# A decoder step on one core: the convolution's state transposed in by 4 blocks of 88 rows and out by 5, in place of 22 and 22

## The chip, the core and the metric

The kernel runs on 1 core of one Trainium2 chip. The core has a matrix engine (TensorE, PE in the rows; PEld is its weight load), three engines for elementwise work (VectorE is DVE, ScalarE is ACT, GpSimd is POOL) and a queue engine that issues transfers (SyncE, SP). Matrix products land in PSUM, everything else lies in SBUF. The metric is the time of one execution on the device in microseconds.

## What is computed

One inference step of a single decoder layer for a prompt of 512 tokens and 8 sampled sequences of 8 tokens (576 tokens together): RMSNorm, one input projection that feeds retention heads and dilated attention heads, an output projection with residual, RMSNorm, a gated feed-forward with a causal depthwise convolution of width 3, and a last RMSNorm. The part that the change touches is the feed-forward with its convolution state:

```python
    h = _rmsnorm(x, norm2_w)
    ua, ub = jnp.split(h @ w_up, [D_FF], axis=-1)
    buf = jnp.concatenate([conv_s0.astype(ua.dtype), ua], axis=1)
    conv = conv_b
    for j in range(CONV_W):
        conv = conv + buf[:, j:j + T] * conv_w[j]
    x = x + (jax.nn.silu(conv) * ub) @ w_down
    return (x, ret_s.astype(ret_s0.dtype), k_all[:, -keep:], v_all[:, -keep:], buf[:, -(CONV_W - 1):])
```

`conv_s0` is `state_conv`, 8 sequences of 2 rows of 2816 features (zero for the prompt). The last two rows of `buf` are an output: 2 rows for the prompt, 16 for the samples.

## The kernel before, in words

Activations are kept with features on the 128 partitions and the 576 tokens along the free side. So 2816 features are 22 tiles (`NF`), numbered f. Every large product goes through `dense` (line 245): for each k tile of the contraction it issues six matmuls (line 254), three passes (high part by high part, high by low, low by high) over two halves of 288 tokens. Weights come 128 columns at a time into `wraw` (three buffers, loaded by SP, line 211), ScalarE makes the high part `whi` (line 219) and VectorE the low part `wlo` (line 229), two buffers each; VectorE's subtraction is what frees a `wraw` buffer for the next load.

The order of work on TensorE is written by `Merge` (line 96) at build time. Each piece of work is a generator that yields an estimated cost and a latency; a stream comes up again once the planner's clock has passed its latency. One k step of `dense` counts 738 ns on that clock. So a stream that yields a latency of 7600 is continued after 11 k steps, one that yields 25000 after 34. Once built, the order is fixed: an engine waits at an instruction whose input is late, and all that is queued behind it on that engine waits too.

When attention and retention are done, the tiles of the last phase are allocated (lines 1018 to 1027) and two streams begin: `conv_state_in` and `rest`, which is `out_proj` (8 tiles of columns, m = 0 to 7, 8 k steps each, with `out_post` behind each) and then `feed_forward` (up f = 0 to 10, down 0 to 7, up f = 11 to 21, down 0 to 7). The first of the new tiles to be filled are `nfw` (line 1285, a 512 KB load) and `csn` (line 1051, the state), both issued by SP ahead of the weights of out tiles m = 3 to 7.

`conv_state_in` loads the state as 16 rows of 2816 floats. 22 transposes of 16 x 128 (line 1055) put it into one PSUM tile, and one VectorE copy (line 1056) brings it to `csT`, [128 features, f, 16]. `up_post` (line 1116) copies a slice of `csT` into the work buffer `ue` on POOL (line 1121), and copies the last two columns of each sequence into `cout` on POOL (lines 1127 and 1128). In the same POOL queue stands the product of gate and convolution (line 1141), which waits for VectorE (line 1138). `conv_state_out` starts in the second run of down products: 22 transposes of `cout[:, f]`, 128 x 18 (line 1160), in groups of four, a VectorE copy behind each group (line 1161), and two stores by SP (lines 1163 and 1164). In `down_post`, `rows_out` transposes the final rows, five transposes for each tile of columns (line 1170).

Of the kernel before, what the change touches and what calls it, by code (L numbers as in the profile page):

```python
# [10 lines left out]
F32 = mybir.dt.float32  # L11
# [7 lines left out]
P = 128  # L19
# [76 lines left out]
class Merge:  # L96
    """Interleaves streams of tensor-engine work.

    A stream is a generator; it yields (cost, latency): what its last burst holds the tensor engine for,
    and how long the other engines then take before its next burst can start.  A third number, if given,  # L100
    takes the place of the cost in the pace.  None: it waits for another stream.  Streams with work
    left advance in proportion to it; a stream without goes first as soon as it is ready."""

# [43 lines left out]
def decoder_step(ctx, tc, a):  # L147
# [14 lines left out]
    def room(n):  # L162
        """n of the small tiles of PSUM are free from here on; give() returns them when their readers are issued"""
        while held[0] + n > 4:
            yield None
        held[0] += n

    def give(n):
        held[0] -= n
# [6 lines left out]

    # ---- weights, streamed in order of use
    def wsrc(w, m, k0, k1):
# [66 lines left out]
    def dense(ps, key, xhi, xlo, k0, k1, first, last, rows=None, made=None):  # L245
        """ps[:, C0 + n] (+)= sum over k of w[k, cols]^T x[k, n], in three exact-split passes."""
        i, (hi, lo) = w_next(key)
        w_split_hi(i + 1)
        for k in range(k0, k1):
            while made is not None and k not in made:  # L250
                yield None
            for wt, x in ((hi, xhi), (hi, xlo), (lo, xhi)):
                for s in range(2):
                    pe.matmul(ps[:, C0 + s * H2:C0 + (s + 1) * H2], wt[:, rows[k] if rows else k - k0], x[k][:, s * H2:(s + 1) * H2],  # L254
                              start=first and k == k0 and wt is hi and x is xhi,
                              stop=last and k == k1 - 1 and wt is lo)
            if k == k0 + 1:
                w_split_lo(i + 1)
            if k == k0 + 3:
                w_load(i + 4)  # L260
            yield 738.0, 0.0
# [3 lines left out]

    # ---- constants
    ident = cst.tile([P, P], F32, name="ident")
# [30 lines left out]
    def rsqrt_steps(dst, v, t):  # L298
        """dst = v ** -0.5 for positive v: a seed from the exponent, then Newton's steps; t: scratch."""
        dve.tensor_scalar(dst.bitcast(I32), v.bitcast(I32), -0.5, 1597463007.0, op0=OP.mult, op1=OP.add)  # L300
        for _ in range(3):
            yield 0.0, 700.0
            dve.tensor_mul(t, dst, dst)
            dve.scalar_tensor_tensor(t, t, -0.5, v, op0=OP.mult, op1=OP.mult)
            dve.scalar_tensor_tensor(dst, t, 1.5, dst, op0=OP.add, op1=OP.mult)
# [17 lines left out]

    # ================= first norm
    def halves():
# [113 lines left out]
    def in_first():  # L439
        """the first two tiles of columns advance together as x arrives"""  # L440
        ps = [dtile() for _ in range(2)]
# [32 lines left out]

    # ================= input projection, retention and dilated attention, by pairs of heads
    mid = ctx.enter_context(ExitStack())
# [12 lines left out]
    def natural(src, dst):  # L489
        """dst [token, tile, 128] = the transpose of src [128 features, T]"""  # L490
        yield from room(2)
        p1, p2 = mtile(), mtile()
        for j in range(5):
            r, s = rows_of(j)
            pe.transpose((p1[:, s] if j < 4 else p2[:NS, :P]), src[:, s], ident)  # L495
        yield 550.0, 300.0
        act.copy(dst[:, 0:4], p1.rearrange("p (j c) -> p j c", j=4))
        dve.tensor_copy(dst[:NS, 4], p2[:NS, :P])
        give(2)
# [91 lines left out]

    # ---- retention
    sbds, s0s, qms = [], [], []
# [11 lines left out]
    def retention():  # L605
        for hp in range(4):
# [5 lines left out]
            for h2, q in halves():  # L612
# [6 lines left out]
                               onehot[:NS, None, :, None].to_broadcast([NS, 2, B, DH]), op=OP.mult)  # L619
            # scores, transposed: [key, query]  # L620
            at = rp.tile([P, 2, 4, P], F32, name="at", tag="at", bufs=1)
# [17 lines left out]
            yield 2 * 216.0, 0.0  # L639
            # states after each chunk  # L640
            yield from room(1)
# [10 lines left out]
            for h2, q in halves():  # L652
                act.activation(st[q], pS[q, q], AF.Copy, scale=fin[q, 0, hp:hp + 1])
            # outputs
            give(1)
# [19 lines left out]
            yield 6 * 216.0, 0.0  # L675
            # group norm; the decay of a row only scales its statistics
            g = gst[hp % 2]
# [25 lines left out]
            for r_, n0, n1_, ps in parts:  # L703
                dve.tensor_mul(cen[:r_, n0:n1_], cen[:r_, n0:n1_],
                               g2[:r_, n0:n1_].unsqueeze(2).to_broadcast([r_, n1_ - n0, DH]))
            # states of the sample group
            yield from room(1)
# [9 lines left out]
            act.activation(sn, sn, AF.Copy, scale=fin[:, 1, hp:hp + 1])  # L717
            # gate
            yield from room(2)
# [11 lines left out]

    # ---- dilated attention, prompt
    half, used = {}, {}
# [7 lines left out]
    def attn_unit(hp, i):  # L741
        """128 queries of two heads, from their scores in PSUM on"""
        n = (i + 1) * P
        S, PT = [], []
        if i:
            # the scores in two passes: [q hi; q hi] with [k hi; k lo], then q lo with k hi
            q_ = A[hp][4][:, i * P:(i + 1) * P]
# [70 lines left out]
    def k_split(hp):  # L818
        """[k hi; k lo] of each head"""
        k_ = A[hp][5]  # L820
# [24 lines left out]

    # ---- dilated attention, sample: four sequences at a time, each in 32 columns of the tensor engine
    kvb = []
    SW = SK + NS

    def attn_sample():  # L850
# [3 lines left out]
        def load(u, x, which):  # L854
            """the 768 rows of a cache that some query of the window reads, for a pair of heads"""
            hp, g = units[u]
# [25 lines left out]
        def unit(u):  # L882
# [19 lines left out]
            dve.tensor_scalar(s[:, :SK], s[:, :SK], c[:, 2:3], None, op0=OP.mult)  # L902
            # the weights of the new tokens, each sequence's in its own 8 of the 64 columns
            dve.tensor_tensor(s[:, SK:].rearrange("p (b t) -> p b t", b=B),
# [95 lines left out]
    kvb.append(kvx.enter_context(tc.tile_pool(name="kv", bufs=2, reuse_waits="tile")))  # L1000
    # the mixed heads take the place of x, in the order in which the output projection takes them
    MIX = [4, 5, 6, 7, 0, 1, 2, 3]
# [13 lines left out]

    # ================= output projection, second norm
    fp = ctx.enter_context(tc.tile_pool(name="ffn", bufs=1, reuse_waits="tile"))
# [4 lines left out]
    csT = fp.tile([P, NF, 16], F32, name="csT")  # L1023
    cout = fp.tile([P, NF, 18], F32, name="cout")
    nfw = fp.tile([P, D], F32, name="nfw")
# [23 lines left out]
    def conv_state_in():  # L1049
        csn = fp.tile([18, DFF], F32, name="csn", tag="co", bufs=1)  # L1050
        sp.dma_start(csn[:16], a["state_conv"].rearrange("b j f -> (b j) f"))
        yield 0.0, 7600.0
        ps = mtile()
        for f in range(NF):
            pe.transpose(ps[:, f * 16:(f + 1) * 16], csn[:16, f * P:(f + 1) * P], ident[:16, :16])
        dve.tensor_copy(csT.rearrange("p f j -> p (f j)"), ps[:, :NF * 16])
        cs_made.append(1)
        yield 1400.0, 4300.0

# [33 lines left out]

    # ================= feed-forward
    ues = []
# [20 lines left out]
    def up_post(f, pa, pb, done, ghi, glo, made):  # L1116
# [9 lines left out]
        act.activation(c[:, :L], u[:, 0:L], AF.Identity, scale=convw[:, 0, f:f + 1], bias=convb[:, f:f + 1])  # L1126
        pool.tensor_copy(cout[:, f, 0:2], u[:, NP:NP + 2])  # L1127
        pool.tensor_copy(by_seq(cout[:, f, 2:]), seqs(u, TS, 2))
        yield 0.0, 1800.0
# [22 lines left out]
    def conv_state_out():  # L1152
        co = fp.tile([18, DFF], F32, name="co", tag="co", bufs=1)
        while len(up_made) < NF:
            yield None
        for f0 in range(0, NF, 4):
            ps = mtile()
            n = min(4, NF - f0)
            for f in range(f0, f0 + n):
                pe.transpose(ps[:18, (f - f0) * P:(f - f0 + 1) * P], cout[:, f], ident)  # L1160
            dve.tensor_copy(co[:, f0 * P:(f0 + n) * P], ps[:18, :n * P])
            yield n * 110.0, 300.0
        sp.dma_start(a["o_conv_p"][0], co[0:2])
        sp.dma_start(a["o_conv_s"].rearrange("b j f -> (b j) f"), co[2:18])

# [30 lines left out]
    def last_down(ghi, glo, yn):  # L1196
        """the last tile of columns, one group of tokens after the other, so that the first one's norm runs beside the second"""
        m, k0 = KD - 1, NFH
# [124 lines left out]
```

## Time and profile before

| what | value |
|---|---|
| runs shown | 839.37 us median of 3 (834.9 to 840.41) |
| profiled execution, first to last instruction | 838.0 us |
| PE busy | 817.6 us (98%) |
| PEld busy | 775.0 us (92%) |
| DVE busy | 414.1 us (49%) |
| ACT busy | 295.2 us (35%) |
| POOL busy | 148.4 us (18%) |
| PE's share of the chain that ended last | 92% (72% is line 254) |

The median stands 1.37 us over the profiled span; launch and end, which lie around the span, are in it. The rows shown further down come from the same execution. A row of the timeline or of the chain gives the start in us, the length in us, the engine, the line, the operation with out<-in, and how many instructions are merged; an idle time ahead of it stands in brackets with what ended it. Ends of matmuls are modelled, so distances from start to start are the safer measure on PE.

### The profile page before, as it was taken

The page shows a single profiled execution, that of the slowest core. Times are in us where ns is not written, and L with a number is a line of the kernel's source. Part 1 is how long each engine was busy: PE and PEld are TensorE (multiplying, and loading weights), DVE is VectorE, ACT ScalarE, POOL GpSimd, SP SyncE. Part 2 cuts the span into 40 slices and gives each one's busy share as a digit, 9 for nine tenths or more (in the row PEclk, how much of TensorE's full clock was granted, in tenths as well). Part 3 has the DMA queues.
Part 4 walks back from the last instruction along what each step waited for, and adds up shares of the span by engine and source line. Part 5 has one row for each costly group of instructions (what it writes and reads, how often), then busy time and mean ns, then how long its engine had stood idle before and what let it go on. Part 6 is the DMA issues. An engine that isn't in the chain of part 4 may idle for free.

```text
span 838.0 us, 16048 instructions
## 1 busy us (share of the span) xinstructions
PE 817.6 (98%) x6594; PEld 775.0 (92%) x6594; DVE 414.1 (49%) x796; ACT 295.2 (35%) x511; POOL 148.4 (18%) x234
## 2 busy tenths in 40 slices
PE   7999999998999999999999999999999999999995
PEld 6999999886887888999999999999999999999995
DVE  5664655655556456544555455432235545545333
ACT  5322321544536367234223333311223323332222
POOL 1312111020111113022212222100012222210111
PEclk9999999999999999899999999999999999999999
DMA  9355562667796873555256544453334445553213
GB/s 268 104 167 163 162 201 70 184 187 217 201 251 184 237 201 85 109 176 169 84 179 198 176 158 138 135 170 87 94 101 156 146 152 176 170 169 81 70 51 114
DMA packets 179534, 128.68 MB, mean 154 GB/s; under 512 B 15425, under 2 KB 176101, under 8 KB 178914
## 3 DMA queue, kind: packets, MB, share of 16 engines
q1 hardware_dynamic: 178308, 93.75, 40.1%
q10 hardware_dynamic: 928, 33.63, 11.0%
q8 instruction: 52, 0.85, 0.4%
q0 software_dynamic: 224, 0.28, 0.1%
q14 instruction: 22, 0.18, 0.1%
HBM read 121.52 MB, written 39.66 MB: 192 GB/s over the span
## 4 chain that ended last, share of the span: by engine, by line
PE 92%; DMA 3%; DVE 1%; ACT 1%; SPq 1%; issue 1%; POOL 0%; ACTq 0%; DVEq 0%; POOLq 0%
PE d L254 72%; PE m L877 2%; PE d L451 2%; PE m L923 2%; DMA kc<-in_cache_win_k_dram 1%; PE m L791 1%; PE d L887 1%; PE m L495 1%; PE m L804 1%; PE px L410 1%; PE m L1213 1%; PE px L254 1%; DMA csn<-in_state_conv_dram 1%; PE m L663 1%; PE m L764 1%
## 5 line engine op out<-in xcount | busy, mean ns | idle before, releaser
L219 ACT ACTIVATE whi<-wraw 128x1024 fp32r<-128x1024 f32 (+2 forms) x114 | 110.8, 972 | 372.2 <-issue 182.1
L229 DVE TENSOR_TENSOR wlo<-wraw,whi 128x1024 fp32r<-128x1024 f32 (+2 forms) x114 | 126.8, 1112 | 119.8 <-ACT whi L219 116.8
L254 PE MATMUL d<-bhi,whi 128*128 128x288 f32 x768 | 174.6, 309 | 0.0
L254 PE MATMUL d<-bhi,wlo 128*128 128x288 f32 x768 | 165.0, 297 | 0.0
L254 PE MATMUL d<-blo,whi 128*128 128x288 f32 x768 | 164.8, 296 | 0.0
L254 PE MATMUL d<-hhi,whi 128*128 128x288 f32 x704 | 150.9, 296 | 0.0
L254 PE MATMUL d<-hlo,whi 128*128 128x288 f32 x704 | 150.8, 296 | 0.0
L254 PE MATMUL d<-hhi,wlo 128*128 128x288 f32 x704 | 150.7, 296 | 0.0
L254 PEld LDWEIGHTS d<-bhi,whi 128*128 128x128 f32 x768 | 122.4, 191 | 5.3 <-issue 3.6
L254 PEld LDWEIGHTS d<-bhi,wlo 128*128 128x128 f32 x768 | 124.1, 189 | 0.0
L254 PEld LDWEIGHTS d<-blo,whi 128*128 128x128 f32 x768 | 124.1, 190 | 0.0
L254 PEld LDWEIGHTS d<-hhi,whi 128*128 128x128 f32 x704 | 113.4, 189 | 0.1
L254 PEld LDWEIGHTS d<-hhi,wlo 128*128 128x128 f32 x704 | 113.4, 189 | 0.0
L254 PEld LDWEIGHTS d<-hlo,whi 128*128 128x128 f32 x704 | 113.4, 189 | 0.0
L1122 DVE TENSOR_TENSOR ue<-d,rstd_b 128x512 f32<-128x512 f32 x22 | 15.2, 691 | 74.5 <-PE d L254 74.5
L1141 POOL TENSOR_TENSOR g<-g,cv 128x512 f32<-128x512 f32 x20 | 25.8, 1290 | 142.5 <-DVE g L1138 137.1
L785 POOL TENSOR_SCALAR s<-s,sc 128x128 f32<-128x128 f32 (+3 forms) x32 | 18.2, 578 | 141.7 <-DVE sc L783 140.4
L1038 POOL TENSOR_TENSOR acc<-acc,sq 128x576 f32<-128x576 f32 x13 | 21.4, 1646 | 111.5 <-ACT sq L1037 111.5
L1127 POOL COPY cout<-ue 128x2 f32<-128x2 f32 x22 | 5.7, 259 | 137.6 <-DVE ue L1122 137.6
L877 PE MATMUL m<-ident,kc 128*128 128x128 f32 x192 | 27.5, 277 | 2.1 <-DMA kc<-in_cache_win_k_dram 2.1
L878 DVE COPY kt<-m 128x384 f32<-128x384 f32 x32 | 17.8, 556 | 23.2 <-PE m L877 22.6
L878 ACT COPY kt<-m 128x384 f32<-128x384 f32 x32 | 15.3, 477 | 38.5 <-PE m L877 38.0
(261 smaller groups left out, 1033.7 us busy)
## 6 DMA issues: line engine op xcount, KB each, us to landing
wraw<-in_w_up_dram SPq DMA_DIRECT2D x44, 512.0 KB
wraw<-in_w_in_dram SPq DMA_DIRECT2D x26, 512.0 KB
kc<-in_cache_win_k_dram SPq DMA_DIRECT2D x32, 256.0 KB
vc<-in_cache_win_v_dram SPq DMA_DIRECT2D x32, 256.0 KB
wraw<-in_w_down_dram SPq DMA_DIRECT2D x16, 384.0 KB
wraw<-in_w_down_dram SPq DMA_DIRECT2D x16, 320.0 KB
kc<-in_cache_win_k_dram SPq DMA_DIRECT2D x64, 64.0 KB
vc<-in_cache_win_v_dram SPq DMA_DIRECT2D x64, 64.0 KB
```

Of the source, the lines that this page charges most:

```text
L219: act.activation(split[i][0][:, c], raw[i][:, c], AF.Copy)
L229: dve.tensor_sub(lo[:, c], raw[i][:, c], f32(hi[:, c]))
L254: pe.matmul(ps[:, C0 + s * H2:C0 + (s + 1) * H2], wt[:, rows[k] if rows else k - k0], x[k][:, s * H2:(s + 1) * H2], start=first and k == k ...
L410: pe.transpose(ps[:, s], xn[:r, j, k * P:(k + 1) * P], ident[:r, :r])
L451: pe.matmul(ps[i][:, C0 + s * H2:C0 + (s + 1) * H2], wt[:, k], x[k][:, s * H2:(s + 1) * H2], start=k == 0 and wt is hi and x is xhis, stop ...
L785: pool.tensor_scalar(s[:, :n], s[:, :n], c[:, 2:3], 1.0, op0=OP.mult, op1=OP.mult)
L877: pe.transpose(ps[:, j * P:(j + 1) * P], K[u, x][:, 3 * w + j], ident)
L878: (act.copy if w else dve.tensor_copy)(kt[:, w * 384:w * 384 + 384], ps[:, :384])
L923: pe.matmul(ps[x * 32:(x + 1) * 32, :P], pt[:n, j, x * 32:(x + 1) * 32], v, start=j == 0, stop=j == 6, tile_position=(0, x * 32))
L1038: pool.tensor_tensor(acc, acc, sq, op=OP.add)
L1122: dve.tensor_mul(u[:, 2:NP + 2], ya[:, :NP], rstd_b[:, :NP])
L1141: eng.tensor_tensor(g[:, :NP], g[:, :NP], c[:, :NP], op=OP.mult)
```

## The change

`csn` becomes [88, 4, 128]. The state, 8 x 2 x 2816 floats, is read as 352 rows of 128 (row number = 22 times the state row + f), 88 rows for each of 4 blocks, so that 4 transposes of 88 x 128 take the place of 22. The copy to `csT` now turns [j, f] into [f, j] as it writes. The latency that the stream yields goes from 7600 to 25000. `cout` changes from [128, f, 18] to [128, 18, f]; the POOL copies write with a step of 22 floats. On the way out the 18 x 22 columns are one flat row of 396, taken as 4 blocks of 88 columns (the samples) and one of 44 (the prompt): 5 transposes, 2 VectorE copies, and the two stores write rows of 128 floats. The rest of the diff takes out comments and docstrings, with blank lines in their places; lines behind 1150 shift by one.

```diff
-    cout = fp.tile([P, NF, 18], F32, name="cout")
+    cout = fp.tile([P, 18, NF], F32, name="cout")
...
     def conv_state_in():
-        csn = fp.tile([18, DFF], F32, name="csn", tag="co", bufs=1)
-        sp.dma_start(csn[:16], a["state_conv"].rearrange("b j f -> (b j) f"))
-        yield 0.0, 7600.0
+        csn = fp.tile([88, 4, P], F32, name="csn", tag="co", bufs=1)
+        sp.dma_start(csn, a["state_conv"].rearrange("b j (f p) -> (b j f) p", p=P).rearrange("(g r) p -> r g p", g=4))
+        yield 0.0, 25000.0
         ps = mtile()
-        for f in range(NF):
-            pe.transpose(ps[:, f * 16:(f + 1) * 16], csn[:16, f * P:(f + 1) * P], ident[:16, :16])
-        dve.tensor_copy(csT.rearrange("p f j -> p (f j)"), ps[:, :NF * 16])
+        for g in range(4):
+            pe.transpose(ps[:, g * 88:(g + 1) * 88], csn[:, g], ident[:88, :88])
+        dve.tensor_copy(csT.rearrange("p f j -> p j f"), ps[:, :352].rearrange("p (j f) -> p j f", f=NF))
         cs_made.append(1)
-        yield 1400.0, 4300.0
+        yield 440.0, 4300.0
...
-        pool.tensor_copy(cout[:, f, 0:2], u[:, NP:NP + 2])
-        pool.tensor_copy(by_seq(cout[:, f, 2:]), seqs(u, TS, 2))
+        pool.tensor_copy(cout[:, 0:2, f], u[:, NP:NP + 2])
+        pool.tensor_copy(by_seq(cout[:, 2:, f]), seqs(u, TS, 2))
...
     def conv_state_out():
-        co = fp.tile([18, DFF], F32, name="co", tag="co", bufs=1)
+        co = fp.tile([88, 5, P], F32, name="co", tag="co", bufs=1)
         while len(up_made) < NF:
             yield None
-        for f0 in range(0, NF, 4):
-            ps = mtile()
-            n = min(4, NF - f0)
-            for f in range(f0, f0 + n):
-                pe.transpose(ps[:18, (f - f0) * P:(f - f0 + 1) * P], cout[:, f], ident)
-            dve.tensor_copy(co[:, f0 * P:(f0 + n) * P], ps[:18, :n * P])
-            yield n * 110.0, 300.0
-        sp.dma_start(a["o_conv_p"][0], co[0:2])
-        sp.dma_start(a["o_conv_s"].rearrange("b j f -> (b j) f"), co[2:18])
+        flat = cout.rearrange("p r f -> p (r f)")
+        ps, p2 = mtile(), mtile()
+        for g in range(4):
+            pe.transpose(ps[:88, g * P:(g + 1) * P], flat[:, 44 + g * 88:44 + (g + 1) * 88], ident)
+        pe.transpose(p2[:44, :P], flat[:, :44], ident)
+        dve.tensor_copy(co[:, 0:4].rearrange("r g p -> r (g p)"), ps[:88])
+        dve.tensor_copy(co[:44, 4], p2[:44, :P])
+        yield 550.0, 800.0
+        sp.dma_start(a["o_conv_p"].rearrange("a j (f p) -> (a j f) p", p=P), co[:44, 4])
+        sp.dma_start(a["o_conv_s"].rearrange("b j (f p) -> (b j f) p", p=P).rearrange("(g r) p -> r g p", g=4), co[:, 0:4])
```

TensorE at the start of the output projection, before: the transposes of the state stand in tile m = 1, behind its third k step (`bhi`, `blo` are the mixed heads in two parts, x2 the two halves of tokens).

```order
L254 MATMUL d<-bhi,whi 128x288 x2
L254 MATMUL d<-blo,whi 128x288 x2
L254 MATMUL d<-bhi,wlo 128x288 x2
L1055 MATMUL m<-ident,csn 128x16 [waits DMAHW7_49]
L1055 MATMUL m<-ident,csn 128x16 x21
```

In the change four transposes stand in tile m = 4, behind its second k step. The tile begins at the row that waits for DVE and ACT.

```order
L254 MATMUL d<-bhi,whi 128x288 [waits DVE_49,Activation_49]
L254 MATMUL d<-bhi,whi 128x288
L254 MATMUL d<-blo,whi 128x288 x2
L254 MATMUL d<-bhi,wlo 128x288 [waits DVE_49]
L254 MATMUL d<-bhi,wlo 128x288
L254 MATMUL d<-bhi,whi 128x288 x2
L254 MATMUL d<-blo,whi 128x288 x2
L254 MATMUL d<-bhi,wlo 128x288 x2
L1055 MATMUL m<-ident,csn 128x88 [waits DMAHW7_49]
L1055 MATMUL m<-ident,csn 128x88 x3
```

From 11 k steps into the projection they moved to 34, 23 k steps later; the load itself keeps its place in SP's queue.

TensorE in the second run of down products, before: the transposes of `cout` stand in six groups, the first three of which are shown with the k steps between them.

```order
L1160 MATMUL m<-ident,cout 18x128 [waits Pool_49] x4
L254 MATMUL d<-ghi,whi 128x288 [waits Activation_49]
L254 MATMUL d<-ghi,whi 128x288
L254 MATMUL d<-glo,whi 128x288 [waits DVE_49]
L254 MATMUL d<-glo,whi 128x288
L254 MATMUL d<-ghi,wlo 128x288 x2
L1160 MATMUL m<-ident,cout 18x128 [waits Pool_49] x4
L254 MATMUL d<-bhi,whi 128x288 [waits PE_49]
L254 MATMUL d<-bhi,whi 128x288
L254 MATMUL d<-blo,whi 128x288 x2
L254 MATMUL d<-bhi,wlo 128x288 x2
L1160 MATMUL m<-ident,cout 18x128 [waits Pool_49] x4
```

In the change there is one group at the place of the first.

```order
L1159 MATMUL m<-ident,cout 88x128 [waits Pool_49]
L1159 MATMUL m<-ident,cout 88x128 x3
L1160 MATMUL m<-ident,cout 44x128
L254 MATMUL d<-ghi,whi 128x288 [waits Activation_49]
L254 MATMUL d<-ghi,whi 128x288
L254 MATMUL d<-glo,whi 128x288 [waits DVE_49]
```

The five later groups are gone from TensorE's queue, and with them four of six copies from VectorE's.

SP's queue in the same stretch, a piece of the difference (`out_dram<-co` are the two stores of the state).

```order
-L211 DMA wraw<-in_w_down_dram 128x5x128
-L1163 DMA out_dram<-co 2x2816
-L1164 DMA out_dram<-co 16x2816
...
+L1164 DMA out_dram<-co 44x128
+L1165 DMA out_dram<-co 88x4x128
+L211 DMA wraw<-in_w_down_dram 128x5x128
```

The stores moved ahead of one weight load that stood in front of them.

## Rows read from the trace of the kernel before

**Rows 1.** The page: span, and TensorE's granted clock in 40 slices (tenths)

```profile
span 838.0 us, 16048 instructions
...
PEclk9999999999999999899999999999999999999999
```

**Rows 2.** Chain that ended last, whole span: start us, us, what

```profile
288.80 0.80 PE m L877 x6
...
342.44 6.35 DMA csn<-in_state_conv_dram
...
351.05 50.47 PE d L254 x360
...
408.12 349.43 PE d L254 x2622
```

**Rows 3.** Timeline of TensorE around the transposes of the state

```profile
346.92 0.42 PE L254 MATMUL d<-bhi,wlo 128*128 128x288 f32 x2
348.84 2.21 PE L1055 MATMUL m<-ident,csn 16*128 16x16 f32 x22 [1.50 <-DMA csn<-in_state_conv_dram]
350.98 0.85 PE L254 MATMUL d<-bhi,whi 128*128 128x288 f32 x2
...
355.94 0.52 PE L254 MATMUL d<-blo,whi 128*128 128x288 f32 x2
...
356.30 0.43 PE L254 MATMUL d<-bhi,wlo 128*128 128x288 f32 x2
```

**Rows 4.** Timeline of ScalarE: splits of weight tiles to their high part

```profile
357.34 1.06 ACT L219 ACTIVATE whi<-wraw 128x1024 fp32r<-128x1024 f32 x1 [10.15 <-PE d L254]
...
363.74 1.06 ACT L219 ACTIVATE whi<-wraw 128x1024 fp32r<-128x1024 f32 x1 [4.03 <-issue]
...
769.81 0.74 ACT L219 ACTIVATE whi<-wraw 128x640 fp32r<-128x640 f32 x1 [3.08 <-PE d L254]
```

**Rows 5.** Stretches: us, PE, PEld, DVE, ACT, POOL busy, PEclk, DMA share, GB/s

```profile
346.00:348.00 2.00, 1.34 (x11) 1.11 (x9) 1.03 (x1) 1.19 (x2) 0.00 (x0) 1.00 1.10 110
348.00:350.00 2.00, 1.16 (x14) 1.16 (x15) 0.00 (x0) 0.00 (x0) 0.00 (x0) 0.83 1.22 280
...
354.00:356.00 2.00, 2.00 (x10) 2.00 (x10) 0.00 (x0) 0.00 (x0) 0.00 (x0) 0.50 0.01 4
356.00:358.00 2.00, 2.00 (x16) 2.00 (x16) 0.44 (x1) 0.66 (x1) 0.00 (x0) 0.97 0.00 0
...
757.00:764.00 7.00, 7.00 (x60) 6.49 (x59) 4.91 (x8) 1.42 (x2) 0.00 (x0) 1.00 0.16 48
```

**Rows 6.** Chain of waits from 755 to 775 us: state and final rows out

```profile
757.55 0.44 PE m L1160 x4
...
763.47 0.22 PE m L1160 x2
...
772.42 0.55 PE m L1170 x5
```

**Rows 7.** Timeline of SP's queue: weights of out tiles, one down tile

```profile
342.88 23.58 SPq L211 DMA_DIRECT2D wraw<-in_w_out_dram  x5
...
756.06 0.37 SPq L211 DMA_DIRECT2D wraw<-in_w_down_dram  x1
```

**Rows 8.** Timeline of VectorE: copies of the state, a tile's first instruction

```profile
351.08 0.53 DVE L1056 COPY csT<-m 128x352 f32<-128x352 f32 x1 [4.05 <-PE m L1055]
...
363.95 0.76 DVE L1078 TENSOR_TENSOR xT<-d,xT 128x576 f32<-128x576 f32 x1 [3.56 <-PE d L254]
...
758.02 0.68 DVE L1161 COPY co<-m 18x512 f32<-18x512 f32 x1 [1.31 <-PE m L1160]
```

**Rows 9.** POOL's waits (us, times, longest), and two of its copies (ns min/median/max)

```profile
POOL g L1141 <- DVE g L1138: 137.1, 19, 7.8
...
L1128 POOL COPY cout<-ue x22: 198/1279/1282, 409.6 to 744.9; 128x16 f32<-128x16 f32 x22
...
L1121 POOL COPY ue<-csT x22: 188/200/804, 400.0 to 741.3; 128x16 f32<-128x16 f32 x22
```

## The prediction

> **What bounds the kernel now.** I read the page first: a span of 838.0 us in which TensorE is busy nearly throughout, and in the row of its granted clock one slice of forty that is below nine tenths, the 17th, from 335 to 356 us [rows 1]. Then the chain that ended last. It is TensorE almost from end to end; behind 408 us it runs 349 us in line 254 without a break. One transfer late in the program stands in it alone: the load of the convolution's state, `csn`, 6.35 us from its issue at 342.44 [rows 2]. So time that TensorE loses here is lost to the end, and time given back here is given back whole, unless something else is late.
>
> The timeline shows the place closely. A pair of matmuls starts at 346.92; the next thing in the queue is the first of the 22 transposes, which starts at 348.84, released by the load. The first pair behind them starts at 350.98 [rows 3]. The stretches show the clock: 1.00 up to 348, 0.83 from 348 to 350, 0.50 from 354 to 356, 0.97 from 356 to 358 [rows 5]. [...] What TensorE did before it fell: it stood idle for the load and then ran only small transposes.
>
> **What the pause costs.** A tile of the output projection takes 6.40 us at full clock (ScalarE's splits at 357.34 and 363.74, one per tile [rows 4]), and has 24 pairs of matmuls, so a pair takes 0.267 us and a k step 0.80. From 346.92 to 350.98 one pair was due: 4.06 - 0.27 = 3.79 us are lost to idling (347.19 to 348.84, 1.65) and transposing (2.14). From 350.98 to 356.30 eleven pairs start; they should have taken 2.93 us and took 5.32, so the low clock costs 2.39 [rows 3]. The pause costs 6.18 us in all.
>
> **Change, part one: the state comes in later.** The load keeps its place in SP's queue, so it still lands at about 348.8. The transposes now stand 23 k steps further on: 347.19 + 23 x 0.80 = 365.6 us. That is 17 us behind the landing, so TensorE doesn't wait there. All 6.18 us go.
>
> What comes in their place is four transposes of 88 x 128. None like it is in the trace. From above: 128 x 128 transposes of another tile take 0.80 us for six, 0.133 each [rows 2], so 0.53. From below: the old ones took 2.21 / 22 = 0.10 each, most of it at half clock [rows 3], so 0.05 each at full clock and 0.20 for four. I take the nearest row in kind, 0.55 us for five transposes of final rows, 0.11 each [rows 6]: 0.44. The result of part one is -5.74.
>
> Other edits of this part I cost at nothing. The load is 352 rows of 512 bytes in place of 16 long ones; it has those 17 us. VectorE's copy writes with a step; it took 0.53 [rows 8] and stands in VectorE's queue ahead of the low part of `h` for tile 3 and the addition of tile 4. VectorE idles 3.56 us of each tile [rows 8], so it may take 4 us without holding anything. Nobody needs `csT` before the up projection, after 400 us [rows 9].
>
> What is late next? The weights of out tiles 3 to 7 are issued from 342.88 on, behind `nfw` and `csn` [rows 7]. With the pause gone TensorE reaches tile 2 at 347.19 + 5 x 0.80 = 351.2 in place of 357.3, and tile 3 at 357.6. There the high part of its weights must be ready, a split of 1.06 us [rows 4], so they have to land by 356.5. The DMA engines are full up to about 352 and at 0.01 from 354 on [rows 5]: whatever was in flight had landed by then. At least 2.5 us are left, and tile 3 is the first of the five. I take nothing.
>
> **Part two: the state goes out.** Five groups of 0.44 and one of 0.22 stand in the chain, 2.42 us for 22 transposes [rows 6]. A block of 18 columns costs 0.11 there, as much as a block of 128 in the rows of five for 0.55. So the price goes by the number of transposes: five cost 0.55. From below, at the 0.05 of part one, it is 0.25, from above, at 0.133, 0.67. I take 0.55, so this part gives -1.87.
>
> The copies on VectorE go from six to two; the first took 0.68, 0.64 after its group began [rows 8], and nothing on TensorE waits for them. On SP the stores now stand ahead of one weight load, issued at 756.06 before [rows 7]. The stores wait for two copies, some 0.64 + 0.68 + 0.3 behind a group that began at 757.38, and take two issues of about 0.4: the load goes out near 759.8, 3.7 us later. Its tile is split at 769.81 [rows 4], 1.9 earlier with the transposes gone, so 8 us are left for landing, where `csn` behind 512 KB took 6.35. Nothing. Loads behind it no longer wait for the sixth copy.
>
> POOL's copies into `cout` write with a step of 22 floats. The nearest row is the copy out of `csT`, 16 elements written in pairs into the spread columns of `ue`: median 0.20 us, with others to 0.80. The present copy takes 0.198 at best with a median of 1.279 [rows 9]. In POOL's queue the product at line 1141 stands behind them, and it waits for VectorE 137.1 us over 19 times, 7.2 us each [rows 9]. That hides them; I take nothing.
>
> **Sum.** -6.18 + 0.44 - 2.42 + 0.55 = -7.61 us against the span of 838.0: 830.4. With the ends of the bounds it is -8.2 (0.20 and 0.25) to -7.4 (0.53 and 0.67). The median of the runs stands 1.37 over that span, which I carry over as launch and end: 839.37 - 7.6 = 831.8. The three runs lie 5.5 us apart, more than any term but the first, and no row says which part of the program that is.
>
> **Rivals.**
> *The pause is longer outside the profile.* The load of the state shares its queue with a 512 KB load and three weight tiles, so its landing may scatter, and the changed kernel no longer depends on it. If the whole 1.37 us between median and span is more pause, the gain is 9.0 and the time 830.4. For it: the spread of the runs. Against it: a launch costs something.
>
> *The clock falls again.* The new transposes could draw it down as the old ones seem to: the 2.39 come back, 834.2. Against it: from 757 to 764 all 22 transposes of `cout` and five others stand between k steps, and the clock is 1.00 over the stretch [rows 5]. There no wait stands ahead of them. [...]
>
> *The pause moves to the weights.* If tile 3's weights land later than 356.5, TensorE waits there in place of here, and at worst the 6.18 come back: 839.37 - 1.87 + 0.44 = 837.9. For it: five loads crowd in after 342. Against it: the DMA share of 0.01 from 354.
>
> *Slower: POOL becomes the bound.* If the stepped writes lengthen the two copies of each f by more than the 7.2 us that cover them, every microsecond beyond delays the product and the down projection's input, 20 times. At 8.0 longer that is 16 us: 839.4 - 7.6 + 16 = 848. Against it: the stepped copy of 0.20 us. [...]
>
> That the change doesn't do what it says is excluded: the order shows 4 and 5 transposes, at their new places.
>
> **Numbers.** A change under 1% is about what can't be told from none; for 839.37 the line is at 831.0, less than 1 us below my forecast. Chances: the forecast 0.50, the longer pause 0.36 (in it the forecast's own scatter beyond the line), the clock 0.06, the weights 0.05, POOL 0.03. So faster 0.36, same 0.50 + 0.06 + 0.05 = 0.61, slower 0.03. The range runs from 828.0 (the longer pause at 830.4, less about half of the runs' spread) to 835.0 (the fallen clock's 834.2 and the bounds of the small terms); beyond it lie the weights, POOL and some of the scatter, under 0.2.
>
> **What would show it.** In the changed kernel's trace: no wait of TensorE for `csn`; clock 1.00 over 340 to 360; the four transposes near 365 with about 0.44 us between the pairs around them; one group of five near 750, about 0.55; no new wait ahead of line 254, above all at tile 3, near 357; the copies into `cout` below some microseconds each; a span near 830.4. I am wrong if a wait for `wraw` stands near 357, if the clock row still dips near 350 or 366, or if the span falls and the median doesn't.

## The result, and the profile after

The change takes 832.76 us (median of 6 runs, 831.28 to 834.93) where the kernel before takes 839.21 (6 runs, 834.9 to 841.45). The ratio estimated from all runs is 0.9935, with a 95% interval from 0.9915 to 0.9954 (the two medians divided give 0.9923): 0.65% faster, or 5.5 us with an interval from 3.9 to 7.1. That is clear of no change, and inside the band of 1% that the prediction called no change. The forecast was 831.8 with a range of 828.0 to 835.0. The profiled execution spans 830.8 us, forecast 830.4.

Two lines of the page answer to [rows 1]. The dip in the 17th slice of the clock is gone; the 8 in the last slice lies behind TensorE's last work, which starts at 822.99 us (granted 0.74 from 823 to 825, 0.50 from there on). A slice is 21 us long, so a short fall can hide in a 9: the third line is the stretch from 200 to 202 us of the same execution (columns as in [rows 5]), far ahead of the changed part, where the granted clock is 0.50.

```profile
span 830.8 us, 15970 instructions
...
PEclk9999999999999999999999999999999999999998
...
200.00:202.00 2.00, 2.00 (x44) 1.62 (x38) 1.66 (x6) 0.83 (x4) 0.00 (x0) 0.50 0.81 235
```

The timeline of TensorE where the four transposes now stand (start us, us, engine, line, operation, count) answers to [rows 3]:

```profile
365.80 0.43 PE L254 MATMUL d<-bhi,wlo 128*128 128x288 f32 x2
366.07 0.47 PE L1055 MATMUL m<-ident,csn 88*128 88x88 f32 x4
366.33 0.52 PE L254 MATMUL d<-bhi,whi 128*128 128x288 f32 x2
366.68 0.43 PE L254 MATMUL d<-blo,whi 128*128 128x288 f32 x2
```

No wait stands in brackets. From 365.80 to 366.33 one pair of 0.27 was due, so the four transposes cost 0.26 us; the pair behind them takes 0.35 to the next start, 0.08 more than the usual 0.27, which makes 0.34. The old place, in the same columns as [rows 5] (us, then PE, PEld, DVE, ACT and POOL busy, granted clock, DMA share, GB/s), runs through at full clock, and the DMA engines have emptied by 352:

```profile
346.00:348.00 2.00, 2.00 (x17) 2.00 (x16) 1.94 (x3) 1.61 (x3) 0.00 (x0) 1.00 1.18 282
348.00:350.00 2.00, 2.00 (x17) 2.00 (x16) 0.25 (x1) 0.00 (x0) 0.00 (x0) 1.00 1.17 287
...
352.00:354.00 2.00, 2.00 (x17) 2.00 (x16) 1.89 (x3) 2.00 (x3) 0.00 (x0) 1.00 0.09 25
```

The chain that ended last (start us, us, what) shows the output side in one piece; it answers to [rows 6] and to the last lines of [rows 2]:

```profile
366.24 0.30 PE m L1055 x4
366.54 29.61 PE d L254 x222
...
402.76 349.44 PE d L254 x2622
752.20 0.44 PE m L1159 x4
752.64 0.11 PE m L1160
752.75 3.19 PE d L254 x24
755.93 0.55 PE m L1171 x5
756.48 8.73 PE d L254 x66
```

Five transposes take 0.55 us, and the k steps behind them are whole again.

**How the difference is read.** The stretch ahead of the output projection, which the change doesn't touch, is not the same length in every execution: SP issues the load of `nfw` as soon as VectorE's line 532 frees its memory (SP waits 20.8 us for it before and 20.9 after), at 342.00 us before and at 342.50 after, and between 340.8 and 345.5 in the executions below. So each trace is measured from that issue to the start of the unbroken run of 2622 matmuls in the up projection, and from there to the first chain row of 66 matmuls behind both the state's and the first final row's transposes.

| execution | `nfw` issued | from there to the run of 2622 | against before | from there to the row of 66 | against before (0: within 0.02) |
|---|---|---|---|---|---|
| before | 342.00 | 66.12 | | 355.56 | |
| the change | 342.50 | 60.26 | -5.86 | 353.72 | -1.84 |
| 22 transposes, later | 341.01 | 60.87 | -5.25 | 355.55 | 0 |
| 4 blocks, old place | 342.32 | 61.09 | -5.03 | 355.55 | 0 |
| output side alone | 343.63 | 64.63 | -1.49 | 353.71 | -1.85 |
| input side alone | 340.79 | 60.27 | -5.85 | 355.55 | 0 |
| 4 blocks, 2 k steps early | 343.53 | 63.69 | -2.43 | 355.56 | 0 |
| 4 blocks, 4 k steps early | 343.73 | 64.39 | -1.73 | 355.58 | 0 |
| 22 transposes, state first | 345.18 | 61.58 | -4.54 | 355.55 | 0 |
| change, state first | 345.47 | 60.27 | -5.85 | 353.70 | -1.86 |

Before and after: +0.50 in front, -5.86 on the input side, -1.84 on the output side, together the 7.2 us between the spans.

### The profile page after: what moved, and what is told of

Same layout as the page of the kernel before. It is cut to its first block, busy times and chain, and to the rows that moved or that the text cites. A ratio compares the mean times of both kernels' runs of the same rounds, so it can differ in the third digit from the quotient of the medians.

```text
span 830.8 us, 15970 instructions
## 1 busy us (share of the span) xinstructions
PE 813.8 (98%) x6559; PEld 772.2 (93%) x6559; DVE 412.5 (50%) x792; ACT 295.3 (36%) x511; POOL 148.0 (18%) x234
## 4 chain that ended last, share of the span: by engine, by line
PE 96%; ACT 1%; DVE 1%; DMA 0%; POOL 0%; issue 0%; ACTq 0%; DVEq 0%; POOLq 0%
PE d L254 75%; PE m L877 2%; PE m L923 2%; PE d L451 2%; PE m L804 1%; PE d L887 1%; PE m L791 1%; PE m L495 1%; PE px L410 1%; PE m L1214 1%; PE px L254 1%; PE m L663 1%; PE m L764 1%; PE d L910 1%; PE m L766 1%; PE m L627 1%
## 5 line engine op out<-in xcount | busy, mean ns | idle before, releaser
L1141 POOL TENSOR_TENSOR g<-g,cv 128x512 f32<-128x512 f32 x20 | 25.7, 1287 | 142.1 <-DVE g L1138 136.7
L1038 POOL TENSOR_TENSOR acc<-acc,sq 128x576 f32<-128x576 f32 x13 | 20.9, 1607 | 104.2 <-ACT sq L1037 104.2
```

Source lines behind the costliest of these rows:

```text
L1038: pool.tensor_tensor(acc, acc, sq, op=OP.add)
L1141: eng.tensor_tensor(g[:, :NP], g[:, :NP], c[:, :NP], op=OP.mult)
```

## Experiments

### The two parts apart

**Input side alone.** The kernel before with the changed `conv_state_in`; `cout` and `conv_state_out` are as before.

```diff
-        csn = fp.tile([18, DFF], F32, name="csn", tag="co", bufs=1)
+        csn = fp.tile([88, 4, P], F32, name="csn", tag="co", bufs=1)
...
-        yield 0.0, 7600.0
+        yield 0.0, 25000.0
...
```

> The kernel before with the input side alone changed (4 blocks of 88 rows, latency 25000); output side as before. Theory: the whole pause goes, 6.18 us, and four transposes cost 0.3 to 0.44: gain 5.7 to 5.9, a span of 832.2, ratio 0.993; with the output side alone it adds up to what the change gives. Rival (the two parts are not independent, for instance since the output's place in SP's queue matters): the sum of the two differs by more than 1 us from the 7.2 by which the span fell.

Measured: 835.57 us (8 runs) beside 839.82 (29 runs of the kernel before), ratio 0.9943 (0.9923 to 0.9964). The pieces of the trace are -5.85 and 0.

**Output side alone.** The kernel before with the changed layout, copies, transposes and stores of the output.

```diff
-    cout = fp.tile([P, NF, 18], F32, name="cout")
+    cout = fp.tile([P, 18, NF], F32, name="cout")
...
+        for g in range(4):
+            pe.transpose(ps[:88, g * P:(g + 1) * P], flat[:, 44 + g * 88:44 + (g + 1) * 88], ident)
+        pe.transpose(p2[:44, :P], flat[:, :44], ident)
...
```

> The kernel before with the output side alone changed (layout of cout, 5 transposes in one group, two copies, stores of 128 floats); the input side is as before. Theory: 22 transposes for 2.42 us become 5 for 0.55, gain 1.87, a span of 836.1 and a ratio of 0.998; the pause near 347 with its low clock stays. Rival (these transposes are hidden behind something, or the stepped copies on POOL cost as much): no gain, ratio 1.000.

Measured: 838.0 us (12 runs) beside the same 839.82, ratio 0.997 (0.995 to 0.9989). The output piece is -1.85, as forecast. The input piece of the one run and the output piece of the other agree to 0.01 us with those of the whole change, so the parts are independent.

Its input side is unchanged, so the trace is a second execution of the old pause, and it is not like the first:

```profile
348.55 0.42 PE L254 MATMUL d<-bhi,wlo 128*128 128x288 f32 x2
350.44 1.53 PE L1055 MATMUL m<-ident,csn 16*128 16x16 f32 x22 [1.48 <-DMA csn<-in_state_conv_dram]
351.90 0.53 PE L254 MATMUL d<-bhi,whi 128*128 128x288 f32 x2
...
352.84 0.68 PE L254 MATMUL d<-bhi,whi 128*128 128x288 f32 x2
...
356.18 0.42 PE L254 MATMUL d<-blo,whi 128*128 128x288 f32 x2
```

The wait is as long as in [rows 3], but here the 22 transposes ran at full clock (1.53 us in place of 2.21), and the clock fell only after the matmuls had begun again: pairs come at 0.48 from 352.84 on (granted 1.00 from 350 to 352, 0.68 from 352 to 354, 0.50 from 354 to 356). From 348.55 to 351.90 are 3.35 - 0.27 = 3.08 us, and the ten pairs to 356.18 took 4.28 in place of 2.67, 1.61 more: a pause of 4.7 where the profiled execution of before had 6.18. That is the -1.49 of the table's input piece.

### What makes the pause: the wait, the transposes, the clock

**22 transposes, later.** One number changes.

```diff
-        yield 0.0, 7600.0
+        yield 0.0, 25000.0
```

> The kernel before with one number changed: the latency of 7600 becomes 25000, so the 22 transposes of 16 rows keep their form and stand 23 k steps later; load, output side and layout are as before. Theory (the pause is the wait for the load, and the low clock follows from that wait together with what stands right behind it): no wait, clock 1.00 throughout, the 22 transposes cost 0.05 to 0.11 us each at full clock, 1.1 to 2.4 us. From the 6.18 us of the pause that leaves a gain of 3.8 to 5.1 us: a span of 833 to 834.2 beside 838.0, ratio 0.994 to 0.9955. Rival (22 transposes in a row draw the clock down by themselves): the clock row dips near 366 us and only the wait's 1.65 us are gained: a span of 836.4, ratio 0.998.

Measured: 835.55 us (10 runs), ratio 0.995 (0.993 to 0.9969).

```profile
364.32 0.43 PE L254 MATMUL d<-bhi,wlo 128*128 128x288 f32 x2
364.68 1.53 PE L1055 MATMUL m<-ident,csn 16*128 16x16 f32 x22
366.14 0.54 PE L254 MATMUL d<-bhi,whi 128*128 128x288 f32 x2
...
364.00:366.00 2.00, 2.00 (x27) 1.83 (x26) 1.23 (x1) 1.33 (x3) 0.52 (x1) 1.00 0.84 240
366.00:368.00 2.00, 2.00 (x18) 1.97 (x17) 1.26 (x2) 0.00 (x0) 0.89 (x1) 1.00 0.72 201
```

Timeline and stretches: 22 transposes without a wait ahead of them cost 1.82 - 0.27 = 1.55 us, 0.07 each, and the clock stays at 1.00. The rival, that they draw it down by themselves, falls at this place. In the traces this one number brings nine tenths of the input side's gain (5.25 of 5.86); some 0.6 to 0.7 us of that are a quicker pace of the matmuls behind, told at the end. By the medians, 835.55 here and 835.57 for the input side alone, no gain of the four larger transposes can be told.

**4 blocks at the old place.** The kernel before with the state loaded and transposed as in the change, but with the latency of the old one; the output side is as before.

```diff
-        csn = fp.tile([18, DFF], F32, name="csn", tag="co", bufs=1)
+        csn = fp.tile([88, 4, P], F32, name="csn", tag="co", bufs=1)
...
         yield 0.0, 7600.0
```

> The kernel before with the state loaded as 88 rows of 4 blocks and turned by 4 transposes, but at the old place (latency 7600); output side as before. Theory one (the idle time in front decides on the clock): the wait of about 1.65 us stays, four transposes cost 0.3 in place of 2.14, the clock still falls for some 2.4 us of loss: gain 1.8, a span of 836.2, ratio 0.998. Theory two (idle time and a run of small transposes are needed together): wait as above, clock 1.00, gain 1.8 + 2.4 = 4.2, a span of 833.8, ratio 0.995. If the wait itself is gone because 88 rows land sooner than 16, the gain is 5.8 and the span 832.2.

Measured: 836.36 us (12 runs), ratio 0.9971 (0.9951 to 0.9992).

```profile
347.24 0.42 PE L254 MATMUL d<-bhi,wlo 128*128 128x288 f32 x2
348.27 0.53 PE L1055 MATMUL m<-ident,csn 88*128 88x88 f32 x4 [0.60 <-DMA csn<-in_state_conv_dram]
348.58 0.50 PE L254 MATMUL d<-bhi,whi 128*128 128x288 f32 x2
...
342.76 5.46 DMA csn<-in_state_conv_dram
```

Neither theory's time came out, because the wait itself was shorter: 347.51 to 348.27, 0.76 us, since the 88-row load landed 5.46 us after its issue, where the 16-row load took 6.35 [rows 2]. The clock stayed at 1.00 (every stretch from 330 to 376) and the pause cost 1.34 - 0.27 = 1.07. On what lowers the clock this run alone decides nothing. Its median gains 3.5 us where its trace gains 5.0, with a wide interval. In some of its 12 executions the clock may have fallen, but only one was traced, and their mean granted clock (0.992 to 0.997) can't tell: in the last run below, which has no wait for the state, it goes from 0.993 to 0.998, and the change's trace has its fall near 200.

**4 blocks, 2 k steps early.** The wait made longer than the old one, with only four transposes behind it. The difference is against the run with 4 blocks at the old place.

```diff
-        yield 0.0, 7600.0
+        yield 0.0, 6100.0
```

> As the run with 4 blocks at the old place, but the latency is 6100: the four transposes stand 2 k steps earlier, so TensorE arrives 1.6 us sooner and waits about 0.76 + 1.6 = 2.4 us for the load, longer than the 1.65 of the kernel before, with 0.3 us of transposes behind it in place of 2.1. Theory (the idle time alone draws the clock down, the transposes add nothing): the clock row dips to 0.5 behind the wait; the pause costs 2.4 + 0.3 and 1.5 to 2.5 for the clock, 4.2 to 5.2 us. Rival (small transposes behind the wait are needed as well): clock 1.00, and the pause costs 2.7.

Measured: 837.07 us (9 runs), ratio 0.9973 (0.9953 to 0.9994).

```profile
346.85 0.42 PE L254 MATMUL d<-bhi,wlo 128*128 128x288 f32 x2
348.94 0.53 PE L1055 MATMUL m<-ident,csn 88*128 88x88 f32 x4 [1.67 <-DMA csn<-in_state_conv_dram]
349.26 0.55 PE L254 MATMUL d<-bhi,whi 128*128 128x288 f32 x2
...
353.25 0.42 PE L254 MATMUL d<-bhi,whi 128*128 128x288 f32 x2
...
348.00:350.00 2.00, 1.06 (x8) 1.06 (x9) 0.49 (x1) 0.71 (x2) 0.00 (x0) 0.90 1.17 283
350.00:352.00 2.00, 2.00 (x10) 2.00 (x9) 2.00 (x3) 0.00 (x0) 0.00 (x0) 0.50 0.86 207
```

TensorE had nothing from 347.12 to 348.94, 1.8 us; then the clock fell, without the 22 transposes. The low clock cost 1.59 (nine pairs in 3.99 in place of 2.40) and the idle with its transposes 2.14, together 3.73, a little under the theory's 4.2 since the load landed in 4.93 us here.

**4 blocks, 4 k steps early.** Again against the run with 4 blocks at the old place.

```diff
-        yield 0.0, 7600.0
+        yield 0.0, 4600.0
```

> As above with a latency of 4600, 4 k steps earlier than in the kernel before: a wait of about 0.76 + 3.2 = 4.0 us and four transposes of 0.3 behind it. Theory (idle time alone is enough): the clock falls for some microseconds, and the pause costs 4.3 plus 1.5 to 2.5, 6 to 7 us, a span about as before. Rival: clock 1.00 and 4.3 us.

Measured: 839.82 us (9 runs), ratio 1.0006 (0.9987 to 1.0025): by the runs the whole gain is gone. (Its trace is still 1.73 us shorter than that of before, 1.2 of it by the quicker pace told at the end.)

```profile
345.44 0.42 PE L254 MATMUL d<-bhi,wlo 128*128 128x288 f32 x2
349.54 0.82 PE L1055 MATMUL m<-ident,csn 88*128 88x88 f32 x4 [3.67 <-DMA csn<-in_state_conv_dram]
350.08 0.83 PE L254 MATMUL d<-bhi,whi 128*128 128x288 f32 x2
...
353.00 0.42 PE L254 MATMUL d<-bhi,whi 128*128 128x288 f32 x2
```

Idle and transposes cost 4.64 - 0.27 = 4.37 and the low clock 1.32 (six pairs in 2.92 in place of 1.60; granted 0.86, 0.50 and 0.79 in the stretches from 348 to 354): 5.7 us. Of the five traces with a wait for the state (before, output side alone, and these three) the clock fell in all but the one with the shortest, 0.76 us. In the five without such a wait (the change, the input side alone, 22 transposes later, and the two below with the state first) it did not fall there (1.00 in each), with four transposes or with 22. So at this place the traces show a fall only with a wait, of 1.6 us or more, and with four transposes as with 22. Whether a wait of only 1.65 us would have been enough with four transposes was not tried.

The length of the wait does not settle it. In this same trace TensorE waits longer for another load, and the clock stays up (timeline, and the stretch from 280 to 292):

```profile
282.90 0.43 PE L254 MATMUL d<-bhi,wlo 128*128 128x288 f32 x2
285.32 0.97 PE L877 MATMUL m<-ident,kc 128*128 128x128 f32 x6 [1.99 <-DMA kc<-in_cache_win_k_dram]
...
280.00:292.00 12.00, 10.01 (x122) 9.03 (x119) 3.62 (x7) 2.70 (x7) 0.69 (x5) 1.00 0.89 253
```

From start to start, less one pair, that is 2.42 - 0.27 = 2.15 us of idle time without a fall, more than the 1.65 in [rows 3] and the 1.8 of the run before this one, each with a fall. What decides was not tried.

### Where the wait came from

**22 transposes, state first.** The kernel before with its two loads swapped in SP's queue.

```diff
         sp.dma_start(csn[:16], a["state_conv"].rearrange("b j f -> (b j) f"))
+        sp.dma_start(nfw, ...)
         yield 0.0, 7600.0
...
-    sp.dma_start(nfw, ...)
     mg.add(conv_state_in(), None)
```

> The kernel before with the two loads swapped in SP's queue: the state first, the 512 KB of nfw behind it. 16 rows, 22 transposes, old place, old output side. Theory (the wait came from standing in the queue behind nfw and behind what nfw waits for): the load lands before 347 us, TensorE does not wait, the clock stays at 1.00 and the 22 transposes cost 1.5 us as they did at their later place: a pause of 1.5 in place of 6.2 (or 4.7), gain 3.2 to 4.7, ratio 0.995. Rival (the wait is the load's own latency): the wait of 1.65 us and the low clock stay, ratio 1.000. A second rival (22 transposes at this place draw the clock down without a wait): gain of the wait alone, 1.65, ratio 0.998.

Measured: 835.57 us (10 runs) beside 839.68 (29 runs), ratio 0.9963 (0.9942 to 0.9984). SP's queue (timeline) and TensorE:

```profile
336.79 0.33 SPq L1051 DMA_DIRECT2D csn<-in_state_conv_dram  x1
345.18 0.35 SPq L1052 DMA_DIRECT2D nfw<-in_normf_w_dram  x1
...
350.09 0.42 PE L254 MATMUL d<-bhi,wlo 128*128 128x288 f32 x2
350.44 1.53 PE L1056 MATMUL m<-ident,csn 16*128 16x16 f32 x22
351.90 0.53 PE L254 MATMUL d<-bhi,whi 128*128 128x288 f32 x2
```

Ahead of `nfw` the load no longer stands behind `nfw`'s wait for VectorE: it goes out 8.4 us before `nfw`, where it followed it by 0.4. TensorE does not wait, and the transposes cost 1.54 at their old place too, at full clock (1.00 from 338 to 364). The wait was made by the order of two loads in the queue.

**Change, state first.** The changed kernel with the same swap and the old latency of 7600.

```diff
-        yield 0.0, 25000.0
+        sp.dma_start(nfw, ...)
+        yield 0.0, 7600.0
...
-    sp.dma_start(nfw, ...)
```

> The changed kernel whole, with 4 and 5 transposes, but with the old latency of 7600 and the state's load ahead of nfw in SP's queue. Theory (the later place is worth only the wait it avoids, and the earlier load avoids it as well): no wait, clock 1.00, the span and the time of the change, 0.992 to 0.9935 of before. Rival (the later place is worth something of its own): 1 us or more slower than the change. A third outcome, if the nfw load behind delays the weights of tile 3: a wait ahead of line 254 near 357 us.

Measured: 833.63 us (8 runs) beside 839.68, ratio 0.9932 (0.9911 to 0.9952).

```profile
350.38 0.43 PE L254 MATMUL d<-bhi,wlo 128*128 128x288 f32 x2
350.65 0.47 PE L1056 MATMUL m<-ident,csn 88*128 88x88 f32 x4
350.91 0.50 PE L254 MATMUL d<-bhi,whi 128*128 128x288 f32 x2
```

Its pieces are -5.85 and -1.86, those of the change. The later place has no worth of its own that these pieces show; it is one of two ways to have the load landed when TensorE comes. No version here is faster than the change.

## Why the prediction was right, point by point

**What bounds it.** Right. What was taken from TensorE's chain came off the span one for one: 5.86 + 1.84 less the 0.50 by which the untouched front was longer.

**The pause.** That it costs 6.18 us and goes whole was right for the profiled execution: 5.86 + 0.34 = 6.20. Its parts were read rightly as wait, transposes and low clock. As the price of the pause in every execution it is too much: the other trace with the old input side has 4.7, because the fall came later there. The transposes took 1.46 in place of 2.14 and the low clock cost 1.61 in place of 2.39; the wait was nearly the same, 1.62. So the term was taken from one trace, and what the clock adds to it was the mis-sized part. The runs point the same way: the forecast gain of 7.6 us lies above the measured 3.9 to 7.1, and with a pause of 4.7 the same sum of measured pieces gives 4.69 - 0.34 + 1.84 = 6.2, inside it. With two traces of the old pause this is consistent, and not shown.

**The four transposes.** Taken at 0.44, measured at 0.26, or 0.34 with the slower pair behind them, inside the bounds of 0.20 to 0.53. The row of transposes that move 128 columns, 0.11 each, was the wrong neighbour. The number of columns moved does not explain it alone: 88 columns cost 0.065 each here and 16 columns 0.07 (22 transposes, later).

**What was costed at nothing.** Right each time. The copy to `csT` took longer with its step, 0.78 in place of 0.53, and the low part of `h` behind it 1.69 where the tiles of before have 0.81; the idle time in front of tile 4's addition shrank from 3.56 [rows 8] to 2.39, so the cover held with more than 2 us to spare (timeline of VectorE):

```profile
366.69 0.78 DVE L1056 COPY csT<-m 128x352 f32<-128x352 f32 x1
367.31 1.69 DVE L1084 SCALAR_TENSOR_TENSOR hlo<-xT,vec,hhi 128x576 fp32r<-128x576 f32 x1
371.40 0.76 DVE L1078 TENSOR_TENSOR xT<-d,xT 128x576 f32<-128x576 f32 x1 [2.39 <-PE d L254]
```

The weights of tile 3 were split at 351.65, when TensorE came to tile 2, not when the load came: the idle time there is ended by TensorE, and the rival that moves the pause to the weights falls.

```profile
351.65 1.06 ACT L219 ACTIVATE whi<-wraw 128x1024 fp32r<-128x1024 f32 x1 [3.97 <-PE d L254]
```

**The output side.** 1.87 forecast, 1.84 measured, 1.85 alone. For the transposes of `cout`, which move 128 columns, the price does go by their number: 0.11 each, whether 18 of its columns are turned (0.44 for four [rows 6]), 88 (0.44 for four) or 44 (0.11). The weight load that moved behind the stores went out at 754.41, and its tile was split at 762.60, 8.2 us later, as worked out.

**POOL.** The stepped copies cost 0.016 us more at best (0.198 in [rows 9]) and 0.018 more in the median (1.279 there), and the wait that hides them is about as long as before, 136.7 us over 19 times. The rival that ends slower falls. For 16 elements with a step of 88 bytes the rows leave room for no more than those 0.02 us a copy.

```profile
POOL g L1141 <- DVE g L1138: 136.7, 19, 7.8
...
L1128 POOL COPY cout<-ue x22: 214/1297/1304, 404.2 to 739.5; 128x16 f32<-128x16 f32 x22
```

**The clock as a rival.** The text said that the old transposes seemed to draw the clock down. They don't, by themselves: 22 of them without a wait run at 1.00 in two traces, and the clock falls behind an idle stretch of 1.8 us with four. At the two places of the state's transposes no trace shows a fall from them alone. Elsewhere the question is open: the fall near 200 us in the change's trace (0.50 from 200 to 202) came behind transposes and waits of 0.88 and 0.39 us, and no run takes that stretch apart. Two other traces are slow there as well: the 56 matmuls of line 923 take 3.27 us in the change and 3.30 with 22 transposes, state first, where seven traces have 1.84, and with the output side alone the 12 matmuls at 202.47 take 2.73, where the others have 1.58 to 1.60 (chains).

**The carry to the median.** 1.37 us was taken as what lies around the span. Each run of the result has its own span beside its time, and the difference is 1.8 in nearly all of them. So the profiled execution of before took 839.8, somewhat over the median of its time, and the 1.37 mixed two things. It cost 0.4 us of the forecast's 1.0 us of error. Another 0.4 is the front, 0.50 longer, less the 0.09 by which the pieces took off more than forecast (7.70 against 7.61); the last 0.16 is the median of the change over its profiled execution's 832.6. The longer pause outside the profile, the rival with 0.36, has no support: the second trace has a shorter one.

**The spread of the runs.** The prediction left open where the runs of one kernel differ. In the ten traces the point at which `nfw` goes out moves by 4.7 us, from 340.79 to 345.47, while the run of 2622 matmuls takes 349.43 to 349.46 in every one. The row of 56 matmuls at line 923 near 287 us (chain) starts 55.00 to 55.04 us ahead of `nfw`'s issue in all ten, the two with swapped loads among them. So, apart from the pause itself, the scatter that the traces show arises ahead of that row. Its cause was not taken apart.

## What to carry to other kernels

A transfer that stands in the chain of a matrix-bound kernel is priced from start to start of the work around it, and here the price had three parts: the wait (1.65 us before), what ran behind it at low clock (2.14), and the slow matmuls until the clock was back; the last cost 2.39 us in one trace of the old pause, 1.61 in another and nothing behind the shortest wait, so it wants more than one trace. Before work is moved to cover a wait, look at what stands ahead of the load in its queue: here swapping two loads gave the same gain as the later place (-5.85 and -5.86 us on the input side). The transposes of `cout` were priced by their number (22 for 2.42 us became 5 for 0.55), so pack rows until a block is full, and take the price from rows with the same count of moved columns.

## What the runs showed of the hardware

- **Behind a wait of 1.8 us and four transposes the granted clock fell** from 1.00 to 0.50 (4 blocks, 2 k steps early). In one trace of the old pause (output side alone) it fell later: the 22 transposes still ran at full clock, in 1.53 us, and the matmuls behind them began at full clock (1.00 from 350 to 352), 0.94 us ahead of the first slow pair. In the four traces with a fall at this place it stayed low for 3.4 to 6.8 us (worked out from the granted clock of the stretches). It did not fall behind every wait of that length: 2.15 us near 284 (4 blocks, 4 k steps early) passed at 1.00.
- **352 rows of 512 bytes landed sooner than 16 rows of 11 KB** behind the same 512 KB load: 5.46, 4.93 and 5.24 us after the issue in three traces (4 blocks at the old place, 2 and 4 k steps early), against 6.35 and 6.33 in two (before, output side alone). Why was not tried.
- **The same matmuls ran at two paces at full clock.** Behind 22 transposes moved later, 222 matmuls take 29.07 us, behind four they take 29.61; in the run 4 k steps early the pairs also come at 0.26 in place of 0.267, and that gives back 1.2 us of its pause by the table. The quicker pace ends with the output projection: the run of 2622 takes 349.43 and 349.46 us in these two, where the change has 349.44. What sets it stays open.

The chain of the run with 22 transposes later, beside the row of 29.61 above:

```profile
366.21 29.07 PE d L254 x222
```
